# Blockwise transposes on VectorE: four per step everywhere, with the cast and the second part one step behind the last of them

## The chip, the cores and the metric

One core of one Trainium2 chip runs the whole program. The metric is the device time of one execution in microseconds, as the median of several runs. Lower is better.

## The reference

A two-layer decoder trunk on 256 tokens of width 2048, all in float32. Layer 0 mixes with a diagonal complex state-space recurrence (S5) and a gated linear unit, layer 1 with dilated sliding-window attention; each is followed by a SwiGLU feed-forward part, and each matrix product is preceded by an RMS norm.

```python
h = rms_norm(x, a_norm_mix[0])
x = x + s5_mixer(h, ...)            # ends in (z @ w_glu): val * sigmoid(gate)
x = x + swiglu(rms_norm(x, ffn_norm[0]), ffn_w_in[0], ffn_w_out[0])
kv = rms_norm(x, kv_norm) @ w_kv    # one shared K and V
h = rms_norm(x, b_norm_mix[0])
x = x + dilated_mixer(h, k, v, w_q, w_o)   # q = h @ w_q for 3 patterns x 16 heads
x = x + swiglu(rms_norm(x, ffn_norm[1]), ffn_w_in[1], ffn_w_out[1])
return rms_norm(x, final_norm)
```

The weights are about 400 MB, and every weight is used once.

## The kernel before

After the S5 recurrence (about the first 130 us) everything is one stream of matrix products, written by `stream`. The stream is cut into jobs, and a job into steps; a step is one block of 128 rows of the contraction, against 1024 columns of weights. The jobs in order are: `glu` (4 jobs of 16 steps), `fi0` (11 jobs of 16), `fo0` (2 jobs of 44), `kv` (1 job of 16), `wq` (6 jobs of 16), `wo` (2 jobs of 16), `fi1` (11 of 16) and `fo1` (2 of 44).

Products are made to near float32 accuracy with two parts. `split` makes a step's weights into `hi` (a rounded copy, by ScalarE, line 761 or 765) and `lo` (what the rounding left, by VectorE, line 139 or 148). TensorE then does, for each of the two halves `m` of the tokens, six matrix products of 128x512: x-high times hi and lo (lines 783 and 784) and x-low times hi (line 787). So a step is twelve products on TensorE, one `hi` on ScalarE and one `lo` on VectorE. `split` runs LA steps ahead of the products: two steps in `glu`, three from `fi0` on. A `hi` or `lo` buffer comes free when its products are done, so ScalarE usually waits for TensorE before a `hi`. In the first step of a job only m=0 is done, in the second both of the second step and the m=1 left over; the last two steps are arranged likewise, so that the results of m=0 are taken out (`evac`) while TensorE still does m=1.

What a job leaves has to be turned (tokens and channels change places) to be the left operand of a later job. Two ways exist. `x_block` and `t4` let TensorE transpose. `turn` lets VectorE do it: a block of 128x512 needs 16 instructions at line 877, each of which turns four 32x32 squares. After the 16, `parts` makes the two parts: ScalarE casts (line 880), and GpSimd subtracts (line 881). For queries and keys there is no `parts` (dst is None), the transposes write the end result.

The order of the work is fixed by hand. `later(d, f)` puts `f` into the list of the step that is d steps ahead; at the end of a step's products the functions in its list are called, in the order in which they were entered. Each engine runs its instructions strictly in the order of the program text, so what a list holds for ScalarE stands behind the `hi` of the same step and ahead of the `hi` of the next.

`turn` spreads a block's 16 transposes over four groups q of four. With rate 1 there is one group per step. With rate 1.25, used where one `evac` leaves two blocks to turn (`wq` jobs 0 and 3, and the first job of `fo0` and of `wo`), the eight groups of two blocks take six steps, two of which hold two groups. The second half of the tokens, m=1, begins 4 steps after the first (one block) or 7 steps (two blocks). `parts` of a block is entered in the same step as its last group.

The tiles named `scr` are scratch of 128x1024 in two buffers, which m=0 and m=1 of a job take in turn; a tile's buffer is given to the next `scr` when all uses of the old one are done.

Of the kernel before, what the change touches and what calls it, by code (L numbers as in the profile page):

```python
# [100 lines left out]
class Trunk:  # L101
# [766 lines left out]
        self.nc.scalar.copy(dst(0), src)  # L868
        self.tt(dst(1), src, dst(0).bitcast(F32), ALU.subtract)

    def turn(self, d, rate, blocks):

        nc = self.nc

        def some(src, out, q):
            for a in range(4):
                nc.vector.transpose(out[32 * q:32 * q + 32, :, 32 * a:32 * a + 32], src[32 * a:32 * a + 32, :, q, :])  # L877

        def parts(out, dst):
            nc.scalar.copy(dst(0), out)  # L880
            nc.gpsimd.tensor_tensor(dst(1), out, dst(0).bitcast(F32), ALU.subtract)  # L881

        for i, (src, out, dst) in enumerate(blocks):
            src = src.rearrange("p (k q c) -> p k q c", k=4, q=4)
            if len(out.shape) == 2:
                out = out.rearrange("p (k t) -> p k t", k=4)
            for q in range(4):
                self.later(d + int((4 * i + q) / rate), lambda src=src, out=out, q=q: some(src, out, q))
            if dst is not None:
                self.later(d + int((4 * i + 3) / rate), lambda out=out, dst=dst: parts(out, dst))  # L890

    def x_dst(self, b, m):
        xt = self.xt
# [25 lines left out]
    def glu_jobs(self):  # L919
        nc = self.nc  # L920
        jobs = []
        for i in range(4):
            def evac(m, ps, i=i):
                x = self.x
                c = slice(512 * i, 512 * i + 512)
                sg = self.scr()
                sg, o = sg[:, 0:512], sg[:, 512:1024]
                nc.scalar.activation(sg, ps[1], AF.Sigmoid)
                self.tt(sg, ps[0], sg, ALU.mult)
                self.tt(x[:, m, c], x[:, m, c], sg, ALU.add)  # L930
                self.later(1 + m, lambda: nc.scalar.activation(sg, x[:, m, c], AF.Square, accum_out=self.ss[:, m, i:i + 1]))
                self.later(1, lambda: self.turn(1 + 4 * m, 1, [(x[:, m, c], o, self.x_dst(i, m))]))
            jb = dict(ks=list(range(16)), evac=evac, load=self.loader("glu", i),
                      lhs=lambda hl, k, m: self.zv(k // 4, hl)[:, k % 4, 128 * m:128 * m + 128])
            jobs.append(jb)
        jobs[1]["start"] = self.new_xt
        jobs[-1]["end"] = lambda: self.later(4, self.rms)
        return jobs

    def ffn_jobs(self, layer, last):  # L940
        nc, a = self.nc, self.a

        def start():
            self.phase.close()
            if self.LA == 2:
                self.LA = 3
                self.p_w4 = self.ctx.enter_context(self.tc.tile_pool(name="w4", bufs=1))
            self.p_h = self.phase.enter_context(self.tc.tile_pool(name=f"h{layer}", bufs=1))
            self.ht = self.p_h.tile([128, 2, 44, 256], F32R, name=self.nm("ht"))

        def gain():
            self.gf = self.p_xt.tile([128, 2048], F32, tag="xt", name="gf")
            nc.gpsimd.dma_start(self.gf, a["gf"][0].partition_broadcast(128))

        jobs = []
        for i in range(11):
            def evac(m, ps, i=i):
                rm = self.r[:, m:m + 1]
                sh = self.scr()
                sg, h = sh[:, 0:512], sh[:, 512:1024]  # L960
                nc.scalar.activation(sg, ps[0], AF.Silu, scale=rm)
                self.stt(h, ps[1], rm, sg, ALU.mult, ALU.mult)
                ht = self.ht
                self.turn(2 + 4 * m, 1, [(h, sg, lambda hl: ht[:, hl, 4 * i:4 * i + 4, 128 * m:128 * m + 128])])
            jobs.append(dict(ks=list(range(16)), evac=evac, load=self.loader(f"fi{layer}", i),
                             gain=lambda k: self.gcol[:, 16 + 16 * layer + k:17 + 16 * layer + k], lhs=self.xt_lhs()))
        jobs[0]["start"] = start
        for i in range(2):
            jobs.append(dict(ks=list(range(44)), evac=self.res_evac(i, not last),
                             load=self.loader(f"fo{layer}", i),  # L970
                             lhs=lambda hl, k, m: self.ht[:, hl, k, 128 * m:128 * m + 128]))
        if last:
            jobs[-2]["start"] = gain
            jobs[-1]["banks"] = [(0,), (1,)]
        else:
            jobs[-2]["start"] = self.new_xt
            jobs[-1]["end"] = lambda: self.later(4, self.rms)
        return jobs

    def res_evac(self, i, trans):  # L980
        def evac(m, ps):
            x = self.x
            sq = self.sq_end = self.scr()
            if not trans and i == 1 and m == 1:
                return self.finish(ps)
            for b in range(2):
                blk = 2 * i + b
                c = slice(512 * blk, 512 * blk + 512)
                self.tt(x[:, m, c], ps[b], x[:, m, c], ALU.add)

                def square(b=b, blk=blk, c=c):
                    self.nc.scalar.activation(sq[:, 512 * b:512 * b + 512], x[:, m, c], AF.Square, accum_out=self.ss[:, m, blk:blk + 1])
                if trans or i == 0:
                    self.later(1 + m, square)
                else:
                    square()
                if trans and i == 1:
                    if b == 0:
                        self.later(2 + m, lambda: self.x_block(2, m))
                    else:  # L1000
                        self.later(1, lambda c=c: self.turn(1 + 4 * m, 1, [(x[:, m, c], sq[:, 512:1024], self.x_dst(3, m))]))
            if trans and i == 0:
                self.later(1, lambda: self.turn(1 + 7 * m, 1.25, [(x[:, m, 512 * b:512 * b + 512], sq[:, 512 * b:512 * b + 512],
                                                            self.x_dst(b, m)) for b in range(2)]))
            if not trans and i == 0:
                self.later(3 + 2 * m, lambda: self.first_half(m))
                self.later(9, lambda: self.nc.scalar.activation(self.r_end[:, m, 3:4], self.r_end[:, m, 0:1], AF.Sqrt))
        return evac
# [54 lines left out]
    def attn_jobs(self):  # L1063
        nc, a = self.nc, self.a
        s = self
# [17 lines left out]
        def kv_evac(m, ps):  # L1083
            k = s.scr()[:, 0:512]
            r = s.r[:, m:m + 1]
            nc.scalar.activation(k, ps[0], AF.Copy, scale=r)
            nc.scalar.activation(s.v[:, 0, m, :], ps[1], AF.Copy, scale=r)
            s.stt(s.v[:, 1, m, :], ps[1], r, s.v[:, 0, m, :].bitcast(F32), ALU.mult, ALU.subtract)
            s.turn(1 + 4 * m, 1, [(k, s.ktr[:, :, 128 * m:128 * m + 128], None)])

        def head(hd, d):
            kv, e = hd // 4, hd % 4
# [52 lines left out]
        for i, pair in enumerate(QPAIRS):  # L1145
            def q_evac(m, ps, i=i, pair=pair):
                qb = s.scr()
                turns = []
                for b in range(2):
                    g, kv = pair[b] // 4, pair[b] % 4  # L1150
                    q = qb[:, 512 * b:512 * b + 512]
                    nc.scalar.activation(q, ps[b], AF.Copy, scale=s.rq[:, m:m + 1])
                    if kv not in s.qt:
                        s.qt[kv] = s.p_a.tile([128, 3, 4, 256], F32, tag="qt", name=s.nm("qt"))
                    dst = s.qt[kv][:, g, :, 128 * m:128 * m + 128]
                    if pair[b] in ON_VECTOR:
                        turns.append((q, dst, None))
                    else:
                        s.later(1 + m, lambda q=q, dst=dst: t4(q, dst))
                if len(turns) == 2:  # L1160
                    s.turn(1 + 7 * m, 1.25, turns)
                elif turns:
                    s.turn(3 + 4 * m, 1, turns)

            def q_end(i=i):
                if i in done:
                    for e in range(4):
                        head(4 * done[i] + e, (3, 6, 8, 10)[e])
            jobs.append(dict(ks=list(range(16)), evac=q_evac, end=q_end, load=s.loader("wq", i),
                             gain=lambda k: s.gcol[:, 48 + k:49 + k], lhs=s.xt_lhs()))  # L1170
# [41 lines left out]
```

## Time and profile before

| what | us |
|---|---|
| median of 3 runs (2189.7 to 2191.47) | 2190.8 |
| the profiled execution, its own time | 2192.67 |
| its span in the profile | 2190.9 |
| TensorE busy in the span | 2129.8 (97%) |
| VectorE busy | 1523.6 (70%) |
| ScalarE busy | 999.6 (46%) |
| GpSimd busy | 203.6 (9%) |

The mean granted clock of TensorE is 0.993. In the profile PE is TensorE's products, PEld its weight loads, DVE VectorE, ACT ScalarE, POOL GpSimd and SP the queue that issues the weight loads from HBM. A line of the timeline gives the start, the length, the engine, the line of the kernel, the operation and the tiles (out<-in), a count where several follow each other, and in brackets the idle time of the engine before it and what ended that.

### The profile page before, as it was taken

To read this page: it belongs to the slowest core of one execution; us is meant where nothing else is said; L and a number is where in the kernel's file an instruction comes from. 1 tells how busy PE (TensorE), PEld (TensorE's weight loads), DVE (VectorE), ACT (ScalarE), POOL (GpSimd) and SP (SyncE) were. 2 spreads that over 40 slices of the span, in tenths; PEclk is the share of its full clock that TensorE was granted. 3 is DMA by queue.
4 is the path that set the end of the run, shared out by engine and by line. 5 is a ranking of instruction groups with operands and counts; after the bars stand their busy time and mean duration, and the time that the engine had idled before them with its cause. 6 is when DMAs were issued, how large, how long until landed. Compare 5 with 4: busy or idle time off the path is not lost.

```text
span 2190.9 us, 28487 instructions
## 1 busy us (share of the span) xinstructions
PE 2129.8 (97%) x11132; PEld 1754.8 (80%) x11132; DVE 1523.6 (70%) x2621; ACT 999.6 (46%) x1157; POOL 203.6 (9%) x180
## 2 busy tenths in 40 slices
PE   4899999999999999999999999999999999999998
PEld 3678888888888888788888888878888888888886
DVE  8977767776777664746686686787767766774544
ACT  4244455444444443344455545544444444443443
POOL 8930000000000000000000000000000000000000
PEclk9899999999999999999999999999999999999999
DMA  5355555555555555455554454445555555555553
GB/s 184 121 193 191 183 214 186 188 194 208 190 186 196 197 193 194 171 208 186 204 182 152 138 189 154 141 166 192 201 187 197 187 209 187 198 209 195 192 193 133
DMA packets 66839, 404.69 MB, mean 185 GB/s; under 512 B 15248, under 2 KB 16784, under 8 KB 19088
## 3 DMA queue, kind: packets, MB, share of 16 engines
q1 hardware_dynamic: 65696, 397.12, 51.3%
q10 hardware_dynamic: 720, 4.18, 0.5%
q8 instruction: 87, 1.43, 0.3%
q0 software_dynamic: 288, 1.57, 0.2%
q14 instruction: 48, 0.39, 0.1%
HBM read 397.34 MB, written 2.10 MB: 182 GB/s over the span
## 4 chain that ended last, share of the span: by engine, by line
PE 88%; DVE 9%; issue 2%; ACT 1%; DMA 0%; ACTq 0%; DVEq 0%
PE b L784 28%; PE b L783 28%; PE b L787 28%; DVE scr L877 2%; DVE lo L139 1%; DVE b L139 1%; PE b L151 1%; PE b L1100 1%; ACT hi L761 1%; DVE b L553 1%; PE b L1131 1%; DVE b L555 1%; DVE vs L556 1%; DVE hi L554 0%; DVE hi L139 0%
## 5 line engine op out<-in xcount | busy, mean ns | idle before, releaser
L148 DVE SCALAR_TENSOR_TENSOR lo<-raw,gcol,hi 128x1024 fp32r<-128x1024 f32 x464 | 594.6, 1291 | 325.0 <-ACT hi L765 319.1
L783 PE MATMUL b<-hi,xt 128*128 128x512 f32 x1856 | 726.5, 391 | 1.6 <-ACT hi L765 1.4
L784 PE MATMUL b<-lo,xt 128*128 128x512 f32 x1856 | 723.0, 390 | 0.9 <-DVE lo L148 0.9
L765 ACT ACTIVATE hi<-raw,gcol 128x1024 fp32r<-128x1024 f32 x464 | 525.1, 1148 | 399.4 <-PE b L787 378.1
L787 PE MATMUL b<-hi,xt 128*128 128x512 f32 x1856 | 572.3, 390 | 0.0
L139 DVE TENSOR_TENSOR lo<-raw,hi 128x1024 fp32r<-128x1024 f32 x264 | 327.5, 1245 | 284.8 <-ACT hi L761 278.5
L761 ACT CAST hi<-raw 128x1024 fp32r<-128x1024 f32 x264 | 275.0, 1052 | 303.2 <-PE b L787 293.5
L783 PEld LDWEIGHTS b<-hi,xt 128*128 128x128 f32 x1856 | 349.0, 188 | 73.5 <-ACT hi L765 1.8
L784 PEld LDWEIGHTS b<-lo,xt 128*128 128x128 f32 x1856 | 348.9, 188 | 72.7 <-DVE lo L148 1.7
L787 PEld LDWEIGHTS b<-hi,xt 128*128 128x128 f32 x1856 | 348.7, 188 | 72.9
L784 PE MATMUL b<-lo,ht 128*128 128x512 f32 x704 | 274.4, 390 | 2.5 <-DVE lo L139 2.5
L783 PE MATMUL b<-hi,ht 128*128 128x512 f32 x704 | 274.0, 389 | 0.1
L877 DVE STREAM_TRANSPOSE scr<-scr 32x128 f32<-32x128 f32 x704 | 212.9, 302 | 11.4
L787 PE MATMUL b<-hi,ht 128*128 128x512 f32 x704 | 217.1, 389 | 0.0
L784 PEld LDWEIGHTS b<-lo,ht 128*128 128x128 f32 x704 | 132.2, 188 | 31.4 <-DVE lo L139 4.1
L783 PEld LDWEIGHTS b<-hi,ht 128*128 128x128 f32 x704 | 132.2, 188 | 27.7 <-ACT hi L761 0.5
L787 PEld LDWEIGHTS b<-hi,ht 128*128 128x128 f32 x704 | 132.2, 188 | 27.6
L881 POOL TENSOR_TENSOR ht<-scr,ht 128x512 fp32r<-128x512 f32 x44 | 57.0, 1295 | 880.9 <-ACT ht L880 880.9
L880 ACT CAST ht<-scr 128x512 fp32r<-128x512 f32 x44 | 27.3, 621 | 178.6 <-DVE scr L877 178.6
L877 DVE STREAM_TRANSPOSE scr<-x 32x128 f32<-32x128 f32 x320 | 96.8, 302 | 4.9
L881 POOL TENSOR_TENSOR xt<-scr,xt 128x512 fp32r<-128x512 f32 x20 | 25.9, 1295 | 770.3 <-ACT xt L880 642.4
L784 PE MATMUL b<-lo,z 128*128 128x512 f32 x224 | 87.6, 391 | 0.6 <-DVE lo L139 0.6
(207 smaller groups left out, 1462.3 us busy)
## 6 DMA issues: line engine op xcount, KB each, us to landing
raw<-in_fi SPq DMA_DIRECT2D x176, 1024.0 KB, 4.7
raw<-in_fo SPq DMA_DIRECT2D x88, 1024.0 KB, 4.7
raw<-in_wq SPq DMA_DIRECT2D x48, 1024.0 KB, 4.7
raw<-in_glu SPq DMA_DIRECT2D x32, 1024.0 KB, 4.8
raw<-in_wo SPq DMA_DIRECT2D x16, 1024.0 KB, 4.7
raw<-in_kv SPq DMA_DIRECT2D x8, 1024.0 KB, 4.7
xw<-in_xu SPq DMA_DIRECT2D x4, 640.0 KB, 11.0
qp<-in_xr SPq DMA_DIRECT2D x4, 512.0 KB, 9.7
```

The costliest lines, as they stand in the source:

```text
L139: self.nc.vector.tensor_tensor(out, in0, in1, op)
L148: self.nc.vector.scalar_tensor_tensor(out, in0, s, in1, op0, op1)
L151: self.nc.tensor.transpose(out, in_, self.ident[:n, :n])
L553: return [lambda: eng.tensor_tensor(ta, bc(a_[:, 0], sh, [1, 3]), x, mul), lambda: eng.tensor_tensor(tb, bc(a_[:, 1:3], sh, [3]), x[:, ::- ...
L761: nc.scalar.copy(hi, raw)
L765: nc.scalar.activation(hi, raw, AF.Copy, scale=gk)
L783: nc.tensor.matmul(ps[b], xh, hi[:, c], start=first, stop=False)
L784: nc.tensor.matmul(ps[b], xh, lo[:, c], start=False, stop=False)
L787: nc.tensor.matmul(ps[b], xl, hi[:, c], start=False, stop=last)
L877: nc.vector.transpose(out[32 * q:32 * q + 32, :, 32 * a:32 * a + 32], src[32 * a:32 * a + 32, :, q, :])
L880: nc.scalar.copy(dst(0), out)
L881: nc.gpsimd.tensor_tensor(dst(1), out, dst(0).bitcast(F32), ALU.subtract)
```

## The change

`turn` loses its rate. Every block gets one group of four transposes per step, so two blocks take eight steps, and m=1 of a pair begins eight steps after m=0. `parts` is entered one step after the last group. No instruction is added or taken away.

```diff
-    def turn(self, d, rate, blocks):
+    def turn(self, d, blocks):
...
             for q in range(4):
-                self.later(d + int((4 * i + q) / rate), lambda src=src, out=out, q=q: some(src, out, q))
+                self.later(d + 4 * i + q, lambda src=src, out=out, q=q: some(src, out, q))
             if dst is not None:
-                self.later(d + int((4 * i + 3) / rate), lambda out=out, dst=dst: parts(out, dst))
+                self.later(d + 4 * i + 4, lambda out=out, dst=dst: parts(out, dst))
...
             if trans and i == 0:
-                self.later(1, lambda: self.turn(1 + 7 * m, 1.25, [(x[:, m, 512 * b:512 * b + 512], sq[:, 512 * b:512 * b + 512],
-                                                            self.x_dst(b, m)) for b in range(2)]))
+                self.later(1, lambda: self.turn(1 + 8 * m, [(x[:, m, 512 * b:512 * b + 512], sq[:, 512 * b:512 * b + 512],
+                                                      self.x_dst(b, m)) for b in range(2)]))
...
                 if len(turns) == 2:
-                    s.turn(1 + 7 * m, 1.25, turns)
+                    s.turn(1 + 8 * m, turns)
                 elif turns:
-                    s.turn(3 + 4 * m, 1, turns)
+                    s.turn(3 + 4 * m, turns)
```

The other calls of `turn` (in `glu`, `fi0`, `fi1`, `kv` and the last job of `fo0` and `wo`) had rate 1 and only lose the argument.

Three places show what moves. The numbers behind a name count buffers and allocations. The first is ScalarE in a `glu` job, around the cast that ends the turned block of m=1. Before:

```order
L761 CAST hi_148_2126<-raw_137_2022 128x1024
L880 CAST xt_123_1953<-scr_122_1949 128x4x128
L761 CAST hi_150_2148<-raw_137_2022 128x1024
L761 CAST hi_153_2166<-raw_142_2066 128x1024
L761 CAST hi_155_2182<-raw_142_2066 128x1024
```

After:

```order
L761 CAST hi_148_2126<-raw_137_2022 128x1024
L761 CAST hi_150_2146<-raw_137_2022 128x1024
L880 CAST xt_123_1953<-scr_122_1949 128x4x128
L761 CAST hi_153_2166<-raw_142_2064 128x1024
L761 CAST hi_155_2182<-raw_142_2064 128x1024
```

The cast (line 880) now stands behind the `hi` of the next step. It is the same at every block with `parts`.

The second is VectorE in the second job of `fo0`, while the two blocks of m=1 are turned. Before (x8 is two groups in one step):

```order
L139 TENSOR_TENSOR lo_914_7415<-raw_900_7288,hi_913_7414 128x1024
L877 STREAM_TRANSPOSE scr_888_7231<-x_1789 32x4x32 x8
L139 TENSOR_TENSOR lo_917_7441<-raw_905_7332,hi_916_7440 128x1024
L877 STREAM_TRANSPOSE scr_888_7231<-x_1789 32x4x32 x4
L139 TENSOR_TENSOR lo_919_7461<-raw_905_7332,hi_918_7460 128x1024
```

After:

```order
L139 TENSOR_TENSOR lo_917_7431<-raw_905_7326,hi_916_7430 128x1024
L877 STREAM_TRANSPOSE scr_888_7231<-x_1789 32x4x32 x4
L139 TENSOR_TENSOR lo_919_7453<-raw_905_7326,hi_918_7452 128x1024
L877 STREAM_TRANSPOSE scr_888_7231<-x_1789 32x4x32 x4
L139 TENSOR_TENSOR lo_922_7475<-raw_910_7370,hi_921_7474 128x1024
```

The doubled group is gone, and the turn of m=1 begins one step later. The third is VectorE where the last job of `wo` ends and `fi1` begins; the four `x<-b` rows are the additions of that job's results to x, and the `xt<-b` row is the second part of a block that TensorE transposed. Before:

```order
L148 SCALAR_TENSOR_TENSOR lo_1584_11676<-raw_1572_11575,gcol_73,hi_1583_11675 128x1024
L139 TENSOR_TENSOR x_1789<-b_1544_11351,x_1789 128x512
L139 TENSOR_TENSOR x_1789<-b_1545_11352,x_1789 128x512
L139 TENSOR_TENSOR x_1789<-b_1548_11371,x_1789 128x512
L139 TENSOR_TENSOR x_1789<-b_1549_11372,x_1789 128x512
L148 SCALAR_TENSOR_TENSOR lo_1589_11709<-raw_1572_11575,gcol_73,hi_1588_11708 128x1024
L148 SCALAR_TENSOR_TENSOR lo_1594_11725<-raw_1577_11619,gcol_73,hi_1593_11724 128x1024
L139 TENSOR_TENSOR xt_1454_10866<-b_1597_11748,xt_1454_10866 128x4x128
```

After:

```order
L148 SCALAR_TENSOR_TENSOR lo_1584_11666<-raw_1572_11567,gcol_73,hi_1583_11665 128x1024
L139 TENSOR_TENSOR x_1789<-b_1544_11351,x_1789 128x512
L139 TENSOR_TENSOR x_1789<-b_1545_11352,x_1789 128x512
L139 TENSOR_TENSOR x_1789<-b_1548_11371,x_1789 128x512
L139 TENSOR_TENSOR x_1789<-b_1549_11372,x_1789 128x512
L877 STREAM_TRANSPOSE scr_1540_11342<-x_1789 32x4x32 x4
L148 SCALAR_TENSOR_TENSOR lo_1589_11703<-raw_1572_11567,gcol_73,hi_1588_11702 128x1024
L877 STREAM_TRANSPOSE scr_1540_11342<-x_1789 32x4x32 x4
L148 SCALAR_TENSOR_TENSOR lo_1594_11723<-raw_1577_11609,gcol_73,hi_1593_11722 128x1024
L139 TENSOR_TENSOR xt_1454_10866<-b_1597_11748,xt_1454_10866 128x4x128
```

Sixteen steps of turning no longer fit between two `evac`s of a 16-step job: two groups of the old turn (`scr_1540`) now stand behind the additions, one in the last step of `wo` and one in the first of `fi1`, and its last `parts` in the second step of `fi1`.

More of the change, by code (lines that the diff above doesn't have):

```diff
@@ L931, in evac @@
                 self.later(1 + m, lambda: nc.scalar.activation(sg, x[:, m, c], AF.Square, accum_out=self.ss[:, m, i:i + 1]))
-                self.later(1, lambda: self.turn(1 + 4 * m, 1, [(x[:, m, c], o, self.x_dst(i, m))]))
+                self.later(1, lambda: self.turn(1 + 4 * m, [(x[:, m, c], o, self.x_dst(i, m))]))
             jb = dict(ks=list(range(16)), evac=evac, load=self.loader("glu", i),
@@ L963, in evac @@
                 ht = self.ht
-                self.turn(2 + 4 * m, 1, [(h, sg, lambda hl: ht[:, hl, 4 * i:4 * i + 4, 128 * m:128 * m + 128])])
+                self.turn(2 + 4 * m, [(h, sg, lambda hl: ht[:, hl, 4 * i:4 * i + 4, 128 * m:128 * m + 128])])
             jobs.append(dict(ks=list(range(16)), evac=evac, load=self.loader(f"fi{layer}", i),
@@ L1000, in evac @@
                     else:
-                        self.later(1, lambda c=c: self.turn(1 + 4 * m, 1, [(x[:, m, c], sq[:, 512:1024], self.x_dst(3, m))]))
+                        self.later(1, lambda c=c: self.turn(1 + 4 * m, [(x[:, m, c], sq[:, 512:1024], self.x_dst(3, m))]))
             if trans and i == 0:
-                self.later(1, lambda: self.turn(1 + 7 * m, 1.25, [(x[:, m, 512 * b:512 * b + 512], sq[:, 512 * b:512 * b + 512],
-                                                            self.x_dst(b, m)) for b in range(2)]))
+                self.later(1, lambda: self.turn(1 + 8 * m, [(x[:, m, 512 * b:512 * b + 512], sq[:, 512 * b:512 * b + 512],
+                                                      self.x_dst(b, m)) for b in range(2)]))
             if not trans and i == 0:
@@ L1088, in kv_evac @@
             s.stt(s.v[:, 1, m, :], ps[1], r, s.v[:, 0, m, :].bitcast(F32), ALU.mult, ALU.subtract)
-            s.turn(1 + 4 * m, 1, [(k, s.ktr[:, :, 128 * m:128 * m + 128], None)])
+            s.turn(1 + 4 * m, [(k, s.ktr[:, :, 128 * m:128 * m + 128], None)])
         def head(hd, d):
```

## The prediction

> **What bounds the kernel now.** I read the page first: how full TensorE is.
>
> ```profile
> span 2190.9 us, 28487 instructions
> PE 2129.8 (97%) x11132; PEld 1754.8 (80%) x11132; DVE 1523.6 (70%) x2621; ACT 999.6 (46%) x1157; POOL 203.6 (9%) x180
> ```
>
> TensorE is the bound, and it idles 61 us, most of it in the S5 part at the start. This change can only win what TensorE loses in the stream behind. A table by stage shows that loss (columns: stretch, its length, PE busy with the count of matmuls, granted clock, DMA share, GB/s). I chose pairs of equal length, a turned stage and a quiet one.
>
> ```profile
> 880.00:940.00 60.00, 57.37 (x249) 1.00 0.49 175
> 940.00:1000.00 60.00, 60.00 (x266) 1.00 0.55 194
> 1410.00:1470.00 60.00, 55.77 (x235) 0.97 0.47 169
> 1480.00:1540.00 60.00, 60.00 (x267) 1.00 0.54 194
> 150.00:280.00 130.00, 129.39 (x568) 1.00 0.53 191
> 320.00:450.00 130.00, 130.00 (x575) 1.00 0.56 197
> 500.00:700.00 200.00, 200.00 (x884) 1.00 0.54 191
> ```
>
> Undisturbed, a matmul takes 200 us / 884 = 0.226 us, so a step of twelve takes 2.71 us. By count, `fo0` loses 17 matmuls, 3.8 us. The entry from `wo` to `fi1` has 235, of which 4 are short transposes of a block (some 0.4 us together): 231 x 0.226 + 0.4 = 52.6, so 7.4 us are lost. The `glu` stretch loses 7, 1.6 us. The busy column shows less (2.6, 4.2, 0.6), since a stall also hides in a stretched matmul; I go by the counts. The stretch 500 to 700, eleven-job feed-forward with casts of the same kind, loses nothing.
>
> Next, who ends TensorE's idle time in these three stretches (columns: total, times, longest), 880 to 940, then 1410 to 1470, then 140 to 285:
>
> ```profile
> PE b L784 <- DVE lo L139: 2.5, 4, 1.0
> ...
> PE b L784 <- DVE lo L139: 1.8, 3, 0.8
> PE b L783 <- ACT hi L765: 1.4, 1, 1.4
> PE b L784 <- DVE lo L148: 0.9, 1, 0.9
> ...
> PE b L784 <- DVE lo L139: 0.6, 3, 0.2
> ```
>
> It is weights that are late, `lo` above all. Why VectorE is late stands in the timelines of ScalarE and VectorE around the first stall of `fo0`, at 911 us:
>
> ```profile
> 908.17 0.62 ACT L880 CAST xt<-scr 128x512 fp32r<-128x512 f32 x1 [7.21 <-DVE scr L877]
> 908.69 3.90 ACT L761 CAST hi<-raw 128x1024 fp32r<-128x1024 f32 x4
> ```
>
> ```profile
> 905.61 1.23 DVE L139 TENSOR_TENSOR lo<-raw,hi 128x1024 fp32r<-128x1024 f32 x1
> 906.87 1.26 DVE L877 STREAM_TRANSPOSE scr<-x 32x128 f32<-32x128 f32 x4
> 909.77 2.61 DVE L139 TENSOR_TENSOR lo<-raw,hi 128x1024 fp32r<-128x1024 f32 x2 [1.64 <-ACT hi L761]
> 912.31 2.50 DVE L877 STREAM_TRANSPOSE scr<-x 32x128 f32<-32x128 f32 x8
> 914.84 1.23 DVE L139 TENSOR_TENSOR lo<-raw,hi 128x1024 fp32r<-128x1024 f32 x1
> ```
>
> The cast stands 7.21 us at the head of ScalarE's queue for the last transposes, and four `hi` that could have been made go out in a row behind it. VectorE, which was the late engine, then idles 1.64 us for a `hi`. So each cast costs VectorE a bubble (the cast's 0.62 and one `hi`, 3.90 / 4), and the x8 groups put 2.5 + 1.25 = 3.8 us of VectorE work into a step of 2.71.
>
> **The change, part by part.**
>
> *The cast behind the next `hi`.* ScalarE makes `hi` of the next step first, VectorE goes on from the transposes to that step's `lo` at once, and the cast follows. The 1.64 us bubble goes at each such block. ScalarE's wait for transposes in the three stretches (880 to 940, 1410 to 1470, 150 to 285), and over all of the feed-forward:
>
> ```profile
> ACT xt L880 <- DVE scr L877: 26.5, 4, 7.3
> ...
> ACT xt L880 <- DVE scr L877: 26.4, 4, 7.3
> ...
> ACT xt L880 <- DVE scr L877: 23.1, 6, 4.4
> ...
> ACT ht L880 <- DVE scr L877: 178.6, 44, 4.7
> ```
>
> The 178.6 us in `fi0` and `fi1` (44 blocks) are worth nothing: TensorE is at 200.00 of 200 there, weights three steps ahead cover it. The casts themselves, 0.62 us, move by one step; ScalarE has 2.71 - 1.15 us free per step, and the consumers of the turned block come several steps later, except at the entry of `fi1` (below).
>
> *One group per step.* VectorE's step is then 1.23 + 1.26 and two gaps, 2.55 us, under 2.71: it gains 0.16 us per step where it lost 1.1 at an x8. With neither bubble nor double group I expect no stall in the second job of `fo0`: all 3.8 us come back. In `glu` weights are only two steps ahead, but the groups were already four per step, so the bubble alone makes the three stalls, one in each of three jobs. The first of them on TensorE:
>
> ```profile
> 182.54 0.39 PE L783 MATMUL b<-hi,z 128*128 128x512 f32 x1
> 183.14 0.50 PE L784 MATMUL b<-lo,z 128*128 128x512 f32 x1 [0.21 <-DVE lo L139]
> 183.47 0.40 PE L783 MATMUL b<-hi,z 128*128 128x512 f32 x1
> ```
>
> From start to start 0.60 and 0.33 in place of 0.226 each: 0.48 us, three times 1.4 us. The other 0.2 of the 1.6 I leave where it is. Without a bubble of 1.64, a `lo` that came 0.4 us late has more than 1 us to spare.
>
> *`wo` to `fi1`.* Of the 7.4 us, part is not idling but a slow clock right behind the stalls:
>
> ```profile
> 1463.60:1466.40 2.80, 2.74 (x7) 0.50 0.77 325
> ```
>
> At clock 0.50 seven matmuls took 2.80 us in place of 7 x 0.226 = 1.6: 1.2 us. I take it that this follows the stalls (1.4 and 0.9 us long) and goes with them. The Trainium skill, "TensorE: Matmul & The Clock Gate" (Part 1), says that the clock halves after an idle window of about 3.4 us; no single wait here is that long, so by that rule the 0.50 would have another cause and could stay, and the gain would be 1.2 us less. The trace has 0.50 nowhere in the quiet stretches above, so I keep the full 7.4.
>
> *What is late next.* In `wo` eight steps per half and two halves make 16 steps of turning in a 16-step job, so two groups and the last cast and subtraction now fall at the entry of `fi1`, ahead of VectorE's and ScalarE's work for x. The entry from `fo0` to `kv` has the same work without the overhang, which gives the price:
>
> ```profile
> 1008.28 2.48 DVE L139 TENSOR_TENSOR x<-b,x 128x512 f32<-128x512 f32 x4
> 1012.57 1.28 DVE L148 SCALAR_TENSOR_TENSOR lo<-raw,gcol,hi 128x1024 fp32r<-128x1024 f32 x1 [0.62 <-ACT hi L765]
> 1016.03 1.28 DVE L148 SCALAR_TENSOR_TENSOR lo<-raw,gcol,hi 128x1024 fp32r<-128x1024 f32 x1 [0.42 <-ACT hi L765]
> 1022.91 1.28 DVE L148 SCALAR_TENSOR_TENSOR lo<-raw,gcol,hi 128x1024 fp32r<-128x1024 f32 x1
> ```
>
> ```profile
> 1027.30 0.39 PE L784 MATMUL b<-lo,xt 128*128 128x512 f32 x1
> ```
>
> The tightest `lo` is that of the eighth step: it ends at 1024.19 and is first used at 1027.30, 3.1 us of room. Two groups cost 2 x 1.29 = 2.6 us, less up to 1.0 of idling (0.62 + 0.42) that they fill. But the squares of x (line 992, for the norm) write a scratch whose old owner is read by the last subtraction on GpSimd: ScalarE waits there for cast 0.62 and subtraction 1.30, and the `hi` behind is late. Followed by hand through the rows, the `lo` comes about 3.1 us later: room about zero. Bounds: no stall if the idling is filled and the wait covered, 0.8 us if neither (2.6 + 1.3 - 3.1). I take 0.3, nearer to the lower end, since the idling in the rows is there.
>
> *Queries (`wq` 0 and 3).* The turn of m=1 also ends in the last step of the next job, so that job's `evac` of m=1 may wait on ScalarE for the last group:
>
> ```profile
> 1138.53 2.40 ACT L1152 ACTIVATE scr<-b,rq 128x512 f32<-128x512 f32 x4
> ...
> 1138.66 1.28 DVE L148 SCALAR_TENSOR_TENSOR lo<-raw,gcol,hi 128x1024 fp32r<-128x1024 f32 x1 [0.71 <-ACT hi L765]
> 1142.00 1.28 DVE L148 SCALAR_TENSOR_TENSOR lo<-raw,gcol,hi 128x1024 fp32r<-128x1024 f32 x1 [2.06 <-ACT hi L765]
> ...
> 1149.69 0.39 PE L784 MATMUL b<-lo,xt 128*128 128x512 f32 x1
> ```
>
> The group would end at 1138.66 + 1.28 + 1.26 = 1141.2, while the copies of m=1 start near 1139.7: ScalarE waits 1.5 us, and the next `lo` ends at 1144.8 in place of 1143.28, for a use at 1149.69. It costs nothing. SP's loads follow the buffers and keep their order; 194 GB/s is the quiet stretches' pace already.
>
> *GpSimd beside VectorE.* A subtraction that overlaps a `lo` slows it:
>
> ```profile
> 898.23 1.30 POOL L881 TENSOR_TENSOR xt<-scr,xt 128x512 fp32r<-128x512 f32 x1 [105.36 <-issue]
> ...
> 899.09 1.53 DVE L139 TENSOR_TENSOR lo<-raw,hi 128x1024 fp32r<-128x1024 f32 x1 [1.69 <-ACT hi L761]
> ```
>
> 0.44 us of overlap made the `lo` 0.3 longer than 1.23. After the change the subtraction starts while VectorE is in back-to-back work, so an overlap stays likely; 0.3 us per block is within the room everywhere but at `fi1`, where the range holds it. The Trainium skill, "SBUF — State Buffer" (Who interferes with whom), speaks against the change here: a VectorE instruction with two SBUF inputs and a GpSimd one that reads SBUF exclude each other for a whole instruction. By it a `lo` could lose the full 1.30 us.
>
> **Sum.** 3.8 + 7.4 + 1.4 - 0.3 = 12.3 us. The profiled execution has span 2190.9 of 2192.67 in all; its span equals the median of the runs, 2190.8, within 0.1, so I take the sum off the median: 2178.5 us.
>
> **Rivals.**
>
> 1. *The overhang costs more.* If the wait on GpSimd, the two groups and the port together run through the entry of `fi1` (0.8 from above, 1.3 for a blocked `lo`, and half-clock matmuls of 1.2 us behind such stalls), 3.3 us stay lost in place of 0.3: 2181.5. For it speaks that the room is about zero; against, that the stages ahead no longer arrive late.
>
> 2. *GpSimd blocks a `lo` at each block* (the rule just named). Where room is over 1.3 us nothing changes; in `glu`, with about 1 to spare, 0.3 us at each of 6 blocks and as much at four of `fo0`: 3 us, 2181.5. Against it: 0.44 of overlap cost only 0.3.
>
> 3. *VectorE's own rate is the limit*, and the bubbles only sit in its slack. Then one group per step moves the stalls of the pair stages to other steps, and only `glu` gains: 2190.8 - 1.4 = 2189.4, no change that can be told. Against it: 2.55 under 2.71, and the single-block stages at that rate show 200.00 of 200.
>
> 4. *Slower.* The cast now follows a `hi` that waits for TensorE, so it can push the next `hi`. If at each of the 64 blocks (44 + 20) that made TensorE wait, it decides from (12.3 + 4.4) / 64 = 0.26 us per block; at the cast's full 0.62 the loss is 40 us, and the time 2190.8 - 12.3 + 40 = 2218. Against it: 1.15 + 0.62 in a step of 2.71, and weights two or three steps ahead.
>
> **How the numbers follow.** A measurement of this kernel tells about 0.2%, 4.4 us, from no change. Chances: forecast 0.74 (own range 2177 to 2180), rival 1 0.10, rival 2 0.06, rival 3 0.06, rival 4 0.04. Faster by over 0.2% takes the forecast and rivals 1 and 2 (0.90), the same is rival 3 (0.06), slower is rival 4 (0.04). The range runs from 2176.5 (the full 12.6 us without the residue is 2178.2; the three runs before lie up to 1.1 us from their median, and each stretch is counted to one matmul, 0.226 us) to 2183 (rivals 1 and 2 and the same spread).
>
> **What the profile after would show.** Right: in the stages of `fo0`, `wo` and `glu` the counts rise to 266 or 267 in 60 us and 575 in 130; ScalarE's waits for transposes fall from 26 us to a few; no clock of 0.50 behind 1460 us; perhaps one wait of TensorE for `lo` of line 148, under 0.5 us, some eight steps into `fi1`. Wrong: waits for `lo` of line 139 in the middle of these jobs (rival 3), waits at `fi1` with a low clock (rival 1), or new waits for `hi` inside `fi0` and `fi1` (rival 4).

## The result and the profile after

On the same chip the changed kernel takes 2178.86 us (median of 4 runs, 2178.21 to 2180.55), the kernel before 2191.14 us (4 runs, 2189.7 to 2192.69). The ratio is 0.9944 with a 95% interval of 0.9932 to 0.9956: 12.28 us saved, where 12.3 was forecast. Single runs of one kernel lie up to 3 us apart, so an agreement that close is in part luck. The profiled execution after took 2180.55 us with a span of 2178.8; against the span of 2190.9 before, that is 12.1 us.

The page of the profile after, its line of totals:

```profile
span 2178.8 us, 28476 instructions
PE 2124.6 (98%) x11132; PEld 1755.0 (81%) x11132; DVE 1522.7 (70%) x2621; ACT 1015.1 (47%) x1157; POOL 232.0 (11%) x180
```

The matmuls and VectorE's busy time are as before. TensorE's idle time (span less busy) fell from 61 to 54 us; the rest of the gain was inside stretched matmuls. GpSimd's busy time rose by 28 us for the same 180 instructions, which I come back to.

The table by stage, the same stretches as before, with one more at the entry of `fi1` that starts later, because the stream runs earlier by then (columns: stretch, length, PE busy with its count, clock, DMA share, GB/s):

```profile
150.00:280.00 130.00, 130.00 (x574) 1.00 0.55 193
880.00:940.00 60.00, 60.00 (x266) 1.00 0.56 193
940.00:1000.00 60.00, 60.00 (x267) 1.00 0.55 193
...
1430.00:1490.00 60.00, 59.63 (x268) 1.00 0.51 178
```

The same stretch of the kernel before:

```profile
1430.00:1490.00 60.00, 55.77 (x237) 0.97 0.47 172
```

Counted in matmuls of 0.226 us: `glu` 568 to 574, 6 or 1.4 us; `fo0` 249 to 266, 17 or 3.8 us; the entry of `fi1` 237 to 268, 31 or 7.0 us. Together 12.2 us, so the three places hold the whole gain. Measured without windows, from TensorE's start on one job to its start on another (table in the second experiment), it is 1.6, 4.1 and 6.8 us, 12.6 together; the S5 part ended 0.5 us later in the profile after, which leaves the 12.1 us of the spans. The clock of 0.50 is gone. ScalarE's waits for transposes in the three stretches of the prediction fell from 26.5, 26.4 and 23.1 us to 0.6, 2.8 and 1.8.

What is left is one wait of TensorE at the entry of `fi1`. First TensorE's timeline there, then VectorE's `lo` that ends it:

```profile
1469.60 0.39 PE L783 MATMUL b<-hi,xt 128*128 128x512 f32 x1
1470.35 0.50 PE L784 MATMUL b<-lo,xt 128*128 128x512 f32 x1 [0.36 <-DVE lo L148]
1470.69 0.39 PE L783 MATMUL b<-hi,xt 128*128 128x512 f32 x1
```

```profile
1469.01 1.29 DVE L148 SCALAR_TENSOR_TENSOR lo<-raw,gcol,hi 128x1024 fp32r<-128x1024 f32 x1
```

Start to start 0.75 and 0.34 in place of 0.226 each: 0.64 us lost. The `lo` ends at 1470.30 and TensorE starts on it at 1470.35. The wait is in the eighth step, as the prediction placed it.

In `fo0` the order on the two engines now looks like this (ScalarE, then VectorE):

```profile
906.76 1.05 ACT L761 CAST hi<-raw 128x1024 fp32r<-128x1024 f32 x1 [1.61 <-PE b L787]
907.73 0.62 ACT L880 CAST xt<-scr 128x512 fp32r<-128x512 f32 x1
909.53 1.05 ACT L761 CAST hi<-raw 128x1024 fp32r<-128x1024 f32 x1 [1.18 <-PE b L787]
```

```profile
906.44 1.26 DVE L877 STREAM_TRANSPOSE scr<-x 32x128 f32<-32x128 f32 x4
907.85 1.23 DVE L139 TENSOR_TENSOR lo<-raw,hi 128x1024 fp32r<-128x1024 f32 x1
908.99 1.24 DVE L877 STREAM_TRANSPOSE scr<-x 32x128 f32<-32x128 f32 x4
910.62 1.23 DVE L139 TENSOR_TENSOR lo<-raw,hi 128x1024 fp32r<-128x1024 f32 x1 [0.40 <-ACT hi L761]
```

The cast has no bracket: its transposes had ended at 907.70, at the time when the `hi` ahead of it was done. ScalarE's only long waits here are for TensorE, that is, it is early. VectorE goes from the transposes to a `lo` with no bubble of 1.64 us.

### The profile page after: what moved, and what is told of

Read it like the earlier page. It is cut to its first block, busy times and chain, and to the rows that moved or that the text cites. A ratio compares the mean times of both kernels' runs of the same rounds, so it can differ in the third digit from the quotient of the medians.

```text
span 2178.8 us, 28476 instructions
## 1 busy us (share of the span) xinstructions
PE 2124.6 (98%) x11132; PEld 1755.0 (81%) x11132; DVE 1522.7 (70%) x2621; ACT 1015.1 (47%) x1157; POOL 232.0 (11%) x180
## 4 chain that ended last, share of the span: by engine, by line
PE 93%; DVE 6%; issue 0%; ACT 0%; DMA 0%; POOL 0%; DVEq 0%; ACTq 0%
PE b L784 30%; PE b L783 30%; PE b L787 30%; DVE b L139 1%; PE b L151 1%; PE b L1100 1%; DVE b L553 1%; PE b L1131 1%; DVE b L555 1%; DVE vs L556 1%; DVE hi L554 0%; DVE hi L139 0%; DVE vs L139 0%; PE b L1102 0%; PE b L1101 0%
## 5 line engine op out<-in xcount | busy, mean ns | idle before, releaser
L765 ACT ACTIVATE hi<-raw,gcol 128x1024 fp32r<-128x1024 f32 x464 | 533.1, 1151 | 545.6 <-PE b L787 541.5
L881 POOL TENSOR_TENSOR ht<-scr,ht 128x512 fp32r<-128x512 f32 x44 | 76.3, 1734 | 857.6 <-ACT ht L880 857.6
L881 POOL TENSOR_TENSOR xt<-scr,xt 128x512 fp32r<-128x512 f32 x20 | 34.9, 1746 | 754.8 <-ACT xt L880 624.6
L783 PE MATMUL b<-hi,z 128*128 128x512 f32 x224 | 87.4, 390 | 0.0
```

The source lines that it names most:

```text
L765: nc.scalar.activation(hi, raw, AF.Copy, scale=gk)
L783: nc.tensor.matmul(ps[b], xh, hi[:, c], start=first, stop=False)
```

## The experiments

My theory behind the forecast had two halves that the sum did not separate: the bubble that a cast at the head of ScalarE's queue leaves on VectorE, and the doubled groups of transposes. The first two kernels do one half each. "Before" in the ratios is the kernel before on the same chip.

### The cast alone one step later, doubled groups kept

The edit, to the kernel before:

```diff
-                self.later(d + int((4 * i + 3) / rate), lambda out=out, dst=dst: parts(out, dst))
+                self.later(d + int((4 * i + 3) / rate) + 1, lambda out=out, dst=dst: parts(out, dst))
```

> Only the cast and subtraction one step behind; two blocks still take six steps with two doubled groups (rate 1.25). Theory (both the bubble at each cast and the doubled group make VectorE late, the bubble alone decides): VectorE has 16 groups of 1.29 us and 14 lo of 1.26 us in 14 steps of 2.71 us, 38.3 against 37.9 us, so its lag stays about constant and the 3.5 us of room at the start of a pair are not used up: no stall in fo0 and wo, none in glu, and no overhang at the entry of fi1. TensorE in 60 us of fo0 and of wo at 265 or more matmuls; the changed kernel's 0.6 us stall in the eighth step of fi1 is gone; 2178.3 us. Rival (the doubled groups are the cause in the pairs): only glu gains, 1.4 us, 2189.7 us. Rival (each has its half): 2184 us.

Measured: 2179.07 us (5 runs, 2178.77 to 2180.36), ratio 0.9942 (0.993 to 0.9955), not to be told from the full change. By stage:

```profile
150.00:280.00 130.00, 130.00 (x574) 1.00 0.55 194
880.00:940.00 60.00, 60.00 (x266) 1.00 0.56 195
1430.00:1490.00 60.00, 59.42 (x265) 1.00 0.55 193
```

So the shift of the cast by one step carries the gain alone, in all three places. The doubled groups, with 3.8 us of VectorE work in a step of 2.71, stop nothing once the bubble is gone: two of them in six steps are carried by the room of the weights. The only wait of TensorE left is at another step, the second of `fi1`, where the products of m=1 wait for the addition to x (the `lo` ahead of these additions started beside a subtraction on GpSimd and took 1.82 us in place of 1.29; the last section comes back to this). It stands in the place of the residue of the full change:

```profile
PE b L783 <- DVE x L139: 0.6, 1, 0.6
```

### The spacing alone, the cast kept in the step of the last group

```diff
-                self.later(d + 4 * i + 4, lambda out=out, dst=dst: parts(out, dst))
+                self.later(d + 4 * i + 3, lambda out=out, dst=dst: parts(out, dst))
```

(here and in the next three, against the changed kernel)

> Only one group of four per step and eight steps for two blocks; the cast and subtraction stay in the step of the last group. Theory: glu is as before (three stalls of 0.48 us). In a pair each block costs VectorE four steps of 2.55 us and one bubble of 1.64 us, 11.8 us against 10.85 of TensorE, so it falls behind by 1.0 us per block, 4 us over four blocks, with 3.5 us of room: 0 to 1 us of stall at the end of the pair in fo0, and in wo the overhang comes on top of that at the entry of fi1, 1 to 4 us. Sum 2191 - 3.3 - 5 = 2182.7 us, between 2181 and 2185. Rival (the doubled groups alone are the cause): all of fo0 and wo comes back, 2180 us. Rival (the bubble alone): 2189 us or more.

Measured: 2188.4 us (11 runs, 2186.64 to 2188.67), ratio 0.9983 (0.9974 to 0.9992): 3.8 us saved. The expectation was too low by 5.7 us. The table shows where:

```profile
880.00:940.00 60.00, 60.00 (x267) 1.00 0.52 185
1430.00:1490.00 60.00, 55.20 (x239) 1.00 0.46 162
150.00:280.00 130.00, 129.42 (x568) 1.00 0.53 190
```

`fo0` is whole, `glu` keeps its loss, and the entry of `fi1` keeps all but two matmuls of its loss, where I had expected 1 to 4 us to stay. The timelines of ScalarE and VectorE there have the reason:

```profile
1459.25 0.62 ACT L880 CAST xt<-scr 128x512 fp32r<-128x512 f32 x1 [8.87 <-DVE scr L877]
```

```profile
1446.52 1.37 DVE L148 SCALAR_TENSOR_TENSOR lo<-raw,gcol,hi 128x1024 fp32r<-128x1024 f32 x1 [1.75 <-ACT hi L765]
1462.18 1.28 DVE L148 SCALAR_TENSOR_TENSOR lo<-raw,gcol,hi 128x1024 fp32r<-128x1024 f32 x1 [2.97 <-ACT hi L765]
```

The last two groups now overhang into `fi1`, and the cast stands 8.87 us for them at the head of ScalarE's queue with a `hi` of the first steps behind it. VectorE idles 2.97 us for that `hi`, after a bubble of 1.75 us at the block before. The lengths of the jobs tell the stages apart (from TensorE's first product with a `lo` in one job to the first in the next, worked out from its timeline; the `glu` row starts at the third step there that is split):

| us | before | cast alone | spacing alone | full change |
|---|---|---|---|---|
| `glu` and the first job of `fi0` | 192.31 | 190.66 | 192.26 | 190.67 |
| second job of `fo0` | 123.81 | 119.68 | 119.68 | 119.68 |
| second job of `wo` | 46.19 | 43.52 | 43.52 | 43.52 |
| first job of `fi1` | 49.27 | 45.51 | 51.83 | 45.15 |

So the spacing by itself repairs the second job of `fo0`, and that of `wo` too, but the first job of `fi1` takes 2.6 us more than before and eats the 2.7 us won in `wo`. Without the later cast it cannot help at the entry.

The room of each `lo` (from its end to its first use by TensorE, worked out from the two engines' timelines) shows why either half is enough in `fo0`:

| second job of `fo0`, turned steps | room of the `lo`, us |
|---|---|
| before | 3.71, 4.47, 3.52, 3.70, 1.90, 2.21, 1.12, then 0.06 |
| cast alone later | never under 2.36 |
| spacing alone | falls to 0.30, at the last block's end |
| the full change | from 3.71 up to 5.9 |

About 3.7 us of room is there at the start. The doubled groups take part of it and each bubble takes 1.64; only the sum goes through it.

### The squares of x in a tile of their own

To see whether the residue of 0.64 us is the wait for GpSimd that the prediction named, the squares of x (only their sums are used) go to a tile that no one else reads:

```diff
+        self.junk = self.p_c.tile([128, 512], mybir.dt.bfloat16, name="junk")
...
-                    self.nc.scalar.activation(sq[:, 512 * b:512 * b + 512], x[:, m, c], AF.Square, accum_out=self.ss[:, m, blk:blk + 1])
+                    self.nc.scalar.activation(self.junk, x[:, m, c], AF.Square, accum_out=self.ss[:, m, blk:blk + 1])
```

> The changed kernel, with the squares of x for the norm written to a tile of their own (in bfloat16, the sum alone is used) instead of the scratch. Theory: at the entry of fi1 ScalarE waited 1.4 us for GpSimd's last subtraction before the squares could take its scratch, and the hi behind them was late. Without that wait the hi comes 1.9 us earlier, and the 0.6 us stall of TensorE in the eighth step of fi1 is gone: no wait of TensorE for lo of line 148, 2178.3 us. Rival (the two transpose groups behind the additions are the cause): the stall stays at 0.4 us of idling or more, 2178.9 us.

Measured: 2177.41 us (4 runs, 2177.24 to 2179.28), ratio 0.9936 (0.9922 to 0.9949). First the changed kernel at this place, ScalarE, GpSimd and VectorE:

```profile
1457.25 0.62 ACT L880 CAST xt<-scr 128x512 fp32r<-128x512 f32 x1 [2.18 <-DVE scr L877]
1459.72 0.63 ACT L992 ACTIVATE scr<-x 128x512 f32<-128x512 f32 x1 [1.36 <-POOL xt L881]
1460.97 1.14 ACT L765 ACTIVATE hi<-raw,gcol 128x1024 fp32r<-128x1024 f32 x1
```

```profile
1457.95 1.74 POOL L881 TENSOR_TENSOR xt<-scr,xt 128x512 fp32r<-128x512 f32 x1 [12.70 <-ACT xt L880]
```

```profile
1462.13 1.28 DVE L148 SCALAR_TENSOR_TENSOR lo<-raw,gcol,hi 128x1024 fp32r<-128x1024 f32 x1 [1.85 <-ACT hi L765]
```

Then the same work with the squares apart, ScalarE and VectorE (one line of code more, so line numbers are one higher), and the stretch:

```profile
1455.17 0.62 ACT L881 CAST xt<-scr 128x512 fp32r<-128x512 f32 x1 [2.24 <-DVE scr L878]
1456.17 0.63 ACT L993 ACTIVATE junk<-x 128x512 bf16<-128x512 f32 x1
1457.56 1.14 ACT L766 ACTIVATE hi<-raw,gcol 128x1024 fp32r<-128x1024 f32 x1
```

```profile
1458.72 1.28 DVE L148 SCALAR_TENSOR_TENSOR lo<-raw,gcol,hi 128x1024 fp32r<-128x1024 f32 x1 [0.52 <-ACT hi L766]
```

```profile
1430.00:1490.00 60.00, 60.00 (x270) 1.00 0.52 190
```

From the start of the cast to the start of the `hi` it takes 2.39 us in place of 3.72, VectorE's bubble falls from 1.85 to 0.52, and TensorE has no wait at this entry. So without the squares' wait for the subtraction on GpSimd there is no residue. The wait is not the whole of it: the room of the `lo` of the eighth step is 3.1 us with the cast alone later (no overhang), 0.85 with the overhang and the squares apart, and nothing in the changed kernel. The overhang takes 2.3 us of the room and the wait 1.3 (1.9 had been expected); only both together go through it. This version has the lowest time of all, 1.4 us under the changed kernel by the medians, of which the first job of `fi1` accounts for 0.66 (44.49 us in place of 45.15). The intervals overlap, so the time by itself doesn't decide; that the stall is gone is shown by the trace.

### The feed-forward's casts back to where they were

```diff
-    def turn(self, d, blocks):
+    def turn(self, d, blocks, behind=1):
...
-                self.later(d + 4 * i + 4, lambda out=out, dst=dst: parts(out, dst))
+                self.later(d + 4 * i + 3 + behind, lambda out=out, dst=dst: parts(out, dst))
...
-                self.turn(2 + 4 * m, [(h, sg, lambda hl: ht[:, hl, 4 * i:4 * i + 4, 128 * m:128 * m + 128])])
+                self.turn(2 + 4 * m, [(h, sg, lambda hl: ht[:, hl, 4 * i:4 * i + 4, 128 * m:128 * m + 128])], 0)
```

> The changed kernel with the cast and subtraction of the feed-forward blocks (44 in fi0 and fi1) back in the step of the last group; all others one step behind. Theory: these casts were covered by weights three steps ahead, so nothing changes: ScalarE's wait at line 880 for ht is back near 178 us, TensorE at 200.0 of 200 us in 500 to 700, 2178.9 us. Rival (part of the gain comes from the feed-forward blocks): 0.1 us for each, 2183 us.

Measured: 2180.01 us (4 runs, 2179.25 to 2180.66), ratio 0.9946 (0.9932 to 0.9959), the same as the full change. ScalarE's wait in the 44 blocks of `fi0` and `fi1` is back:

```profile
ACT ht L880 <- DVE scr L877: 178.5, 44, 4.7
```

TensorE waits in its stream are those of the changed kernel. So the 178.5 us are worth nothing. Weights there are three steps ahead and the turn has one group per step, as in `fo0` with the spacing alone, which had bubbles and no stall either; `glu`, with weights two steps ahead, stalls (next experiment).

### The casts of `glu` alone back to where they were

The same edit with `behind` at 0 in the call of `glu`:

```diff
-                self.later(1, lambda: self.turn(1 + 4 * m, [(x[:, m, c], o, self.x_dst(i, m))]))
+                self.later(1, lambda: self.turn(1 + 4 * m, [(x[:, m, c], o, self.x_dst(i, m))], 0))
```

> The changed kernel with the cast and subtraction of the glu blocks alone back in the step of the last group. Theory: the bubble alone makes the glu stalls, since weights are only two steps ahead there: the three stalls of 0.48 us are back (TensorE at 568 matmuls in 150 to 280 us, three waits for lo of line 139), all else as in the changed kernel, 2180.3 us. Rival (the glu gain came from elsewhere, or the port of GpSimd): no stall in glu, 2178.9 us.

Measured: 2181.87 us (3 runs, 2180.62 to 2182.07), ratio 0.9956 (0.994 to 0.9972). The stretch and the waits of TensorE:

```profile
150.00:280.00 130.00, 129.43 (x567) 1.00 0.53 192
```

```profile
PE b L784 <- DVE lo L139: 0.6, 3, 0.2
```

The three waits are back, and 7 matmuls are missing again, 1.6 us; by its jobs `glu` is 1.6 us longer than in the changed kernel and everything behind it is the same. The median lies 3.0 us above the changed kernel's, and 1.6 above the 2180.3 expected; with three runs 1.5 us apart and overlapping intervals that difference says no more than the trace does. The bubble alone makes the waits, with four transposes per step throughout.

### Two groups in every step of a pair, the cast later

Does the spacing matter at all, then? From the kernel of the first experiment (cast later), the pairs go to two groups in each of four steps:

```diff
-                self.later(1, lambda: self.turn(1 + 7 * m, 1.25, [(x[:, m, 512 * b:512 * b + 512], sq[:, 512 * b:512 * b + 512],
+                self.later(1, lambda: self.turn(1 + 4 * m, 2, [(x[:, m, 512 * b:512 * b + 512], sq[:, 512 * b:512 * b + 512],
...
-                    s.turn(1 + 7 * m, 1.25, turns)
+                    s.turn(1 + 4 * m, 2, turns)
```

> The cast and subtraction one step behind, and the turns of two blocks pressed into eight steps in a row with two groups in each (rate 2, m=1 four steps behind m=0). Theory (VectorE's rate is a limit, but the weights ahead hold 3.5 to 4.6 us of room): each doubled step costs VectorE 1.1 us of room, eight of them 8.6 us against 4.6 of room in fo0 and wo, so 4 us of stall in each of these, and 9.6 against 4.4 in the two wq pairs, 5 us each; 18 us in all, 2197 us, against 2179 with the groups spread at rate 1.25. Rival (once the bubble is gone the spacing does not matter at all): 2179 us.

Measured: 2197.03 us (8 runs, 2195.77 to 2198.16), ratio 1.0024 (1.0014 to 1.0035), slower than before by the interval, and 18.0 us over the first experiment by the medians (which come from two chips; 19 us with each taken against the kernel before on its own). VectorE in `fo0` has no gap now, and TensorE's count and waits (the whole of `fo0` to the entry of `fi1`) show the price:

```profile
898.68 1.23 DVE L139 TENSOR_TENSOR lo<-raw,hi 128x1024 fp32r<-128x1024 f32 x1
899.94 2.53 DVE L877 STREAM_TRANSPOSE scr<-x 32x128 f32<-32x128 f32 x8
902.50 1.23 DVE L139 TENSOR_TENSOR lo<-raw,hi 128x1024 fp32r<-128x1024 f32 x1
```

```profile
880.00:940.00 60.00, 57.34 (x249) 1.00 0.51 182
```

```profile
PE b L784 <- DVE lo L148: 7.2, 10, 0.9
PE b L784 <- DVE lo L139: 5.4, 8, 0.8
```

From `lo` to `lo` VectorE takes 902.50 - 898.68 = 3.82 us, 1.1 more than TensorE's step of 2.71. Eight such steps in a row take 8.9 us out of a room of about 4. By the lengths of their jobs the four stages with pairs lose 3.9 us (`fo0`), 5.2 and 5.2 (`wq`) and 3.9 (`wo`), 18.2 together, as the expectation had worked out. So spacing is free up to the room, and full price beyond it.

## Why the prediction was right, point by point

- *`fo0`, 3.8 us: right*, 17 matmuls came back, 4.1 us by the length of the job. The prediction charged the loss to the bubble and the x8 groups together and did not part them. The runs do: either one alone stays within the room.
- *Entry of `fi1`, 7.4 less 0.3 us: right as a net, with the residue too small.* The counts gave 31 matmuls, 7.0 us net, the lengths of the jobs 6.8. The term "I take 0.3" was mis-sized: 0.64 us, inside its bounds of 0 to 0.8. Its working had the subtraction at 1.30 us; it took 1.74, and ScalarE's wait for it was not covered. The upper bound itself leaves out the cast of 0.62 us that the working names; with it the bound would be 1.4. The squares in their own tile took the stall away, and so did the run without the overhang: both are needed for it.
- *`glu`, 1.4 us: right,* and the 0.2 us that the sum left where they were came too: 1.6 by the length of the jobs. 6 matmuls came back with the later cast, and 7 went again when only these casts were put back. That the sum hit 12.3 is partly luck: `glu` and `fo0` gave 0.2 and 0.3 us more than forecast and the entry 0.3 less.
- *The feed-forward's 178.6 us worth nothing: right.* With those casts put back the time stayed.
- *Queries at no cost: right.* ScalarE waits for the last group as worked out (1.5 us), and TensorE has no wait in that stretch:

```profile
1135.99 1.27 ACT L1152 ACTIVATE scr<-b,rq 128x512 f32<-128x512 f32 x2 [1.56 <-DVE qt L877]
```

- *The clock of 0.50 goes with the stalls: right.* It went, and between 130 and 2160 us it is in none of the later runs, though some of them stall. Before, TensorE's waits ahead of it were these:

```profile
1460.48 0.51 PE L783 MATMUL b<-hi,xt 128*128 128x512 f32 x1 [1.37 <-ACT hi L765]
1461.86 0.50 PE L784 MATMUL b<-lo,xt 128*128 128x512 f32 x1 [0.87 <-DVE lo L148]
```

With the spacing alone one wait there is longer, and the clock of the stretch is 1.00:

```profile
PE b L783 <- DVE x L139: 1.7, 1, 1.7
```

With two groups per step TensorE waits 18 times, up to 0.9 us, at 1.00 as well. So a long wait by itself does not bring the 0.50 here. What does can be read from the clock: the 0.50 lasts 3.41 us before, and in the S5 part of the traces 3.41 us or a multiple of it. In the 3.41 us ahead of the drop TensorE was busy for 1.60 us, since two waits fell into them; in the 3.41 us around the longer single wait of the spacing alone (third row) it was busy for 1.69 us, and the clock stayed (columns: stretch, length, PE busy with its count, clock, DMA share, GB/s):

```profile
1459.55:1462.96 3.41, 1.60 (x6) 1.00 0.15 22
1462.96:1466.38 3.42, 3.22 (x8) 0.50 0.72 285
...
1450.18:1453.59 3.41, 1.69 (x8) 1.00 0.63 207
```

All eight traces, cut into stretches of 3.41 us at the points where their clock steps, say the same of the stretches at full clock:

| TensorE busy in the stretch | stretches | at 0.50 in the next |
|---|---|---|
| under 0.49 of it | 29 | 29 |
| 0.49 to 0.80 | 46 | 1 (0.56 busy, in the S5 part) |
| over 0.80 | 4890 | 0 |

So in these runs the clock halves for 3.41 us when TensorE was busy for less than about half of the 3.41 us ahead, however the idling is cut up. Where the stretches begin relative to the kernel differs between the profiles (the first 0.50 begins at 49.8 us before and at 50.6 with the cast alone). An estimate from TensorE's rows before: with the cuts laid elsewhere, in about half of the positions no stretch there would fall under 0.49. So the 1.2 us need not be in every execution of the kernel before, and it is in part luck that they came in full. The Trainium skill, "TensorE: Matmul & The Clock Gate" (Part 1), asks for an idle window of about 3.4 us. The length agrees with the 3.41 us here; no single wait at this place is that long, and in these traces a stretch that is 47% busy already counts as idle.
- *GpSimd slows a `lo` by 0.3 us: wrong in who pays.* All but three `lo` kept their length, and the subtraction got longer, as the last section shows. TensorE did not feel it except at the entry of `fi1`, where ScalarE waits for the subtraction.
- *The rivals.* Rival 1 had the place and the mechanism of the residue, but 3.3 us in place of 0.64. Rival 2 would have left waits for `lo` in `glu` and `fo0`: there are none. Rival 3 (VectorE's rate is the limit) falls with the first experiment, in which even the doubled groups pass; the last one shows at which load it would hold. Rival 4 would show waits of TensorE for `hi` in `fi0` and `fi1`. Past the S5 part the whole trace has one wait of TensorE:

```profile
PE b L784 <- DVE lo L148: 0.4, 1, 0.4
```

## What to carry to other kernels

An engine that waits in its queue for a second engine's work, while the second engine next needs something from the first, makes the second idle too; put such a consumer one step behind its producer, and look for the bubble on the late engine (here 1.64 us), not at the length of the wait (178.5 us of it cost nothing here, 23.1 us in `glu` cost 1.6). Whether a burst on the late engine hurts is told by the room of its results, from end to first use: sum what each burst and bubble takes out of it. Where an overhang falls into a crowded entry, look at scratch tiles that a slower engine still reads; a tile of its own took that wait away.

## What the runs showed of the hardware that I had not expected

The subtraction on GpSimd, before and after, beside the `lo` after (groups by line: count, busy us, mean ns, idle before):

```profile
L881 POOL TENSOR_TENSOR ht<-scr,ht 128x512 fp32r<-128x512 f32 x44 | 57.0, 1295 | 880.9 <-ACT ht L880 880.9
```

```profile
L881 POOL TENSOR_TENSOR ht<-scr,ht 128x512 fp32r<-128x512 f32 x44 | 76.3, 1734 | 857.6 <-ACT ht L880 857.6
L148 DVE SCALAR_TENSOR_TENSOR lo<-raw,gcol,hi 128x1024 fp32r<-128x1024 f32 x464 | 596.8, 1288 | 320.3 <-ACT hi L765 312.5
```

Before, it began while VectorE idled in the bubble, and the `lo` that started before its end was the one that took longer. Now it starts while a `lo` runs, and takes 0.44 us more, whereas the `lo` keeps its 1.29 us. With the feed-forward's casts alone put back, the subtractions of those 44 blocks took 1296 ns again and the 20 others 1744. At the entry of `fi1` the subtraction that starts at 1457.95 meets this `lo`:

```profile
1457.25 1.28 DVE L148 SCALAR_TENSOR_TENSOR lo<-raw,gcol,hi 128x1024 fp32r<-128x1024 f32 x1
```

The `lo` ends at 1458.53, so they overlap by 0.58 us, and the subtraction is 0.44 us longer. (VectorE then does a part of 0.68 us beside it, but the price is that of the other rows with the same overlap.) In the prediction's row it was the other way about: the `lo` started while a subtraction ran, overlapped it by 0.44 us, and was 0.3 us longer. All rows of the two traces, worked out from the timelines (a `lo` of line 139 takes 1.23 us by itself, one of line 148 1.285, a subtraction 1.295):

| trace | the second to start | rows | overlap, us | longer by, us | overlap less that |
|---|---|---|---|---|---|
| before | `lo`, line 139 | 17 | 0.38 to 0.44 | 0.24 to 0.30 | 0.14 |
| before | `lo`, line 148 | 47 | 0.26 to 0.29 | 0.06 to 0.09 | 0.20 |
| after | subtraction, beside a `lo` of line 139 | 16 | 0.47 to 0.66 | 0.33 to 0.52 | 0.14 |
| after | subtraction, beside a `lo` of line 148 | 48 | 0.57 to 0.73 | 0.43 to 0.59 | 0.14 |
| after | `lo`, line 148 | 3 | 0.72 to 0.73 | 0.52 | 0.20 |

In every row the one that starts second pays, and it pays the overlap less 0.14 or 0.20 us: it hardly gets on until the first has ended. The Trainium skill, "SBUF — State Buffer" (Who interferes with whom), calls the port pair that the two engines share an exclusive lock; that the first keeps its full speed and the second waits it out agrees with it. What can be lost is so the rest of the first instruction, and not, as Rival 2 took from that rule, more than 1 us at each block: after the change an overlap costs at most 0.6.
